# Routing written out in order, router logits in rounded parts, final norm inside the last expert, merging adds on VectorE

## Chip, cores and metric

One core of a Trainium2 chip. The time is that of one execution on the device, in microseconds (us). Engines are named as in the profile: PE is TensorE, DVE VectorE, ACT ScalarE, POOL GpSimd, SP SyncE; SPq and POOLq are the DMA queues that SyncE and GpSimd issue.

## What is computed

One layer of an encoder, all in float32, 1024 rows (tokens) of 1024 columns:

```python
xn = rms_norm(h, mix_norm_g);  p = xn @ w_in
merged = sum over b in (S5, RG-LRU, GLA) of sigmoid(gate_b) * (mixer_b(p_b) @ w_up_b)
h = h + merged @ w_mix_out
hn = rms_norm(h, ffn_norm_g)
probs = softmax(hn @ w_router)                 # 1024 x 16
gate, idx = lax.top_k(swapaxes(probs, 1, 2), 128)   # each expert takes its 128 best rows
xe = hn[idx]
hid = silu(xe @ w_exp_gate) * (xe @ w_exp_up)  # 1024 -> 2048
ye = (hid @ w_exp_down) * gate
h = h + scatter_add(idx, ye)
out = rms_norm(h, final_norm_g)
```

`rms_norm(h, g)` is `h * rsqrt(mean(h*h) + EPS) * g`, by row.

## The kernel before

A float32 product is made of three products of rounded parts: each operand is split into a high part `hi` (ScalarE's copy into the rounded type) and a low part `lo = x - hi` (VectorE), and `mm3` (L67 to L70) issues `hi*lo`, `hi*hi` and `lo*hi`. Weights are split in the kernel, in tiles of 128x1024, so each costs one ScalarE instruction (`xwh`) and one VectorE instruction (`xwl`).

**Mixers (to 712 us).** Projections and the three mixers; each branch is multiplied by its gate on VectorE and added into `merged` (8 tiles of 128x1024) by `gated` (L661 to L668), whose add went to GpSimd unless `eng` said VectorE. The order of this part is the framework's scheduler's. The LRU takes four blocks of columns through convolution, gates and scan on VectorE, with projections (`pj`) and its own products (`mx`) between them on TensorE.

**Output product (712 to 849).** `half(h, ...)` (L1075 to L1113) goes over the eight row tiles of 128 rows, once for the left 512 columns and once for the right: 24 matmuls of `mix` into `mo`, the add of the residual on VectorE, a write to `HACC` in device memory, squares with row sums on ScalarE, then four transposes `pt` and four float32 products `LG` with the router's weights `wr`. In the second half `route(t)` (L1178 to L1210) follows for each row tile: 12 instructions on 128x1 for the reciprocal root `rs`, the row scaled by it on ScalarE (`hn`), multiplied by the norm's gain `gff` on GpSimd and written to `HN` in device memory, and some 20 instructions of softmax on 128x16, the exponential by a polynomial. `prr` repeats each probability eight times and is transposed into `PT` (an expert in eight partitions).

**Search, slots, first gather (849 to 889).** Ten rounds (L1252 to L1262) find each expert's threshold: VectorE counts over the 1024 rows in `PT` (`junk`, 128x1024), TensorE sums the counts, VectorE sets the next digit. Between the rounds stand the parts of `probs` in bfloat16 (`aux`). Then come slot numbers (`sl`), the first expert's mask (128x1024), the product that turns it into row indices and gates, and the indirect read of its 128 rows from `HN` (`xe`).

**Experts (889 to 1986).** Sixteen experts, twelve operations each of 48 matmuls: `g` (gate), `u` (up), `d` (down) for four blocks of 512 columns, in the order of `SEQ` (L991 to L997). The instruction order is written by hand (`manual_schedule`, L1497 to L1525): `pre` and `post` hold what goes before and behind the matmuls of operation `i`, `NX` is the number of operations. During one operation the four weight tiles of the next are split. Weights come through 15 buffers of 1 MB (`rawa`, `rawb`, `rawc`), each loaded again once its split is done. The results of an expert are added to `HACC` by an indirect write.

**Final norm (1986 to 2015.8).** Four loads bring all of `HACC` back (`fin_load`), the last expert's rows are held apart. Behind the last operation `fin_sq`, `fin_rs`, `fin_out` (L1461 to L1478) go over pairs of row tiles: squares on ScalarE, 11 small instructions of reciprocal root on VectorE, the product with root and gain on VectorE or on ScalarE and GpSimd, the write to `out`. `row_add` adds the last expert's rows, `row_out` (L1485 to L1488) norms them and writes them by an indirect DMA of GpSimd's queue, over the plain rows.

Of the kernel before, what the change touches and what calls it, by code (L numbers as in the profile page):

```python
# [42 lines left out]
def hybrid_encoder(ctx: ExitStack, tc: tile.TileContext, A, out, dbg=None):  # L43
# [1031 lines left out]
    def half(h, H, w, pool, after):  # L1075

        def logits(t):
            pt = bank("pt")
            for j in range(4):
                te.transpose(pt[:, j * P:(j + 1) * P], H(t)[:, j * P:(j + 1) * P], idn)  # L1080
            hT = pool.tile([P, 4, P], F32, name="hT", bufs=2)
            act(hT.rearrange("p a b -> p (a b)"), pt, AF.Copy)
            yield
            for j in range(4):
                te.matmul(LG[:, t], hT[:, j], wr[:, 4 * h + j], start=False, stop=(h == 1 and j == 3),  # L1085
                          skip_group_check=True)
            yield

        lgen = rgen = iter(())
        for t in range(NT):  # L1090
            ps = bank("mo")
            mix(t, w, ps, 0, 2)
            next(lgen, None)
            mix(t, w, ps, 2, 4)
            next(lgen, None)
            if t:
                next(rgen, None)
                rgen = after(t - 1)
                next(rgen, None)
            mix(t, w, ps, 4, KT)  # L1100
            tt(v, H(t), ps, H(t), ADD)
            g.dma_start(HACC[t * P:(t + 1) * P, h * 512:(h + 1) * 512], H(t))
            sq = pool.tile([P, 512], F32, name="sq")
            act(sq, H(t), AF.Square, accum_out=ssq[:, h, t:t + 1])
            lgen = logits(t)
        with tc.manual_schedule():
            for _ in lgen:
                pass
            next(rgen, None)
            for _ in after(NT - 1):  # L1110
                pass

    half(0, lambda t: H0[:, t], wm[0], w0p, lambda t: iter(()))  # L1113
# [13 lines left out]
    bi_ = c2.tile([P, P], I32, name="bi")  # L1127
# [14 lines left out]
    aux = c2.tile([P, NE, NT, 5], BF, name="aux")  # L1142
# [35 lines left out]
    def route(t):  # L1178
        ss_, rs2, tm2, nm, sm_ = (w1p.tile(c1, F32, name=n, bufs=2) for n in ("ss2", "rs2", "tm2", "nm", "sm"))
        tt(v, ss_, ssq[:, 0, t:t + 1], ssq[:, 1, t:t + 1], ADD)  # L1180
        v.tensor_scalar(ss_, ss_, 1.0 / D, EPS, op0=MUL, op1=ADD)
# [394 lines left out]
```

## Time and profile before

| | |
|---|---|
| median of 3 runs | 2017.3 us (2012.62 to 2018.07) |
| profiled execution | 2017.55 us, span 2015.8 us |
| TensorE busy | 1883.6 us (93%) |
| VectorE busy | 1575.1 us (78%) |
| ScalarE busy | 1178.0 us (58%) |
| GpSimd busy | 211.7 us (11%) |
| mean rate of DMA | 246 GB/s |

The profile is of one execution. "Busy" counts the time in which an engine carries out instructions; a number in square brackets behind a row is the time that the engine stood idle before it, and what released it. The stages differ in which engine fills them, so the shares are read by stretch. The numbered groups of rows are further below.

### The profile page before, as it was taken

To read this page: it belongs to the slowest core of one execution; us is meant where nothing else is said; L and a number is where in the kernel's file an instruction comes from. 1 tells how busy PE (TensorE), PEld (TensorE's weight loads), DVE (VectorE), ACT (ScalarE), POOL (GpSimd) and SP (SyncE) were. 2 spreads that over 40 slices of the span, in tenths; PEclk is the share of its full clock that TensorE was granted. 3 is DMA by queue.
4 is the path that set the end of the run, shared out by engine and by line. 5 is a ranking of instruction groups with operands and counts; after the bars stand their busy time and mean duration, and the time that the engine had idled before them with its cause. 6 is when DMAs were issued, how large, how long until landed. Compare 5 with 4: busy or idle time off the path is not lost.

```text
span 2015.8 us, 25693 instructions
## 1 busy us (share of the span) xinstructions
PE 1883.6 (93%) x9502; PEld 1545.1 (77%) x9502; DVE 1575.1 (78%) x2162; ACT 1178.0 (58%) x1381; POOL 211.7 (11%) x227
## 2 busy tenths in 40 slices
PE   7999989999998998549999999999999999999994
PEld 6878866777777877438888888888888888888883
DVE  7467226558766245879999999999999999999997
ACT  5221234435574132327777778777777777777774
POOL 0834000002112102300000000000000000000001
PEclk9989999999999999869999999999999999999997
DMA  5431421302212162949999999999999999999972
GB/s 164 106 98 37 106 82 29 89 20 72 57 44 82 32 218 77 331 161 369 375 383 384 388 381 378 391 383 382 381 391 384 379 382 391 381 381 377 393 291 94
DMA packets 263233, 495.96 MB, mean 246 GB/s; under 512 B 26756, under 2 KB 82468, under 8 KB 263108
## 3 DMA queue, kind: packets, MB, share of 16 engines
q1 hardware_dynamic: 255924, 468.64, 64.4%
q0 software_dynamic: 7184, 25.69, 4.3%
q8 instruction: 74, 1.21, 0.2%
q14 instruction: 51, 0.42, 0.1%
HBM read 464.55 MB, written 29.74 MB: 245 GB/s over the span
## 4 chain that ended last, share of the span: by engine, by line
PE 77%; DVE 9%; ACT 3%; issue 2%; DMA 0%; SPq 0%; POOLq 0%; DVEq 0%; ACTq 0%
PE py L1379 17%; PE gu L68 12%; PE pj L380 12%; PE gu L70 12%; PE gu L69 12%; PE pj L390 3%; PE tp L1335 2%; PE mo L68 1%; PE mo L70 1%; PE mo L69 1%; DVE e L57 1%; DVE junk L1253 1%; DVE xc L57 1%; PE LG L1085 1%; PE mx L795 0%
## 5 line engine op out<-in xcount | busy, mean ns | idle before, releaser
L233 DVE TENSOR_TENSOR xwl<-rawb,xwh 128x1024 fp32r<-128x1024 f32 x528 | 613.7, 1218 | 20.4 <-ACT xwh L54 19.3
L54 ACT ACTIVATE xwh<-rawb 128x1024 fp32r<-128x1024 f32 x528 | 522.0, 1052 | 17.4 <-PE gu L70 7.5
L68 PE MATMUL gu<-xwl,xeh 128*128 128x512 f32 x1024 | 407.5, 398 | 0.0
L70 PE MATMUL gu<-xwh,xel 128*128 128x512 f32 x1024 | 400.3, 391 | 0.0
L69 PE MATMUL gu<-xwh,xeh 128*128 128x512 f32 x1024 | 399.1, 390 | 0.0
L233 DVE TENSOR_TENSOR xwl<-rawa,xwh 128x1024 fp32r<-128x1024 f32 x192 | 226.1, 1218 | 17.3 <-ACT xwh L54 17.3
L70 PEld LDWEIGHTS gu<-xwh,xel 128*128 128x128 f32 x1024 | 192.5, 188 | 41.9 <-DVE xel L62 0.3
L69 PEld LDWEIGHTS gu<-xwh,xeh 128*128 128x128 f32 x1024 | 193.1, 189 | 38.1
L68 PEld LDWEIGHTS gu<-xwl,xeh 128*128 128x128 f32 x1024 | 192.7, 188 | 37.4 <-ACT xeh L54 0.2
L54 ACT ACTIVATE xwh<-rawa 128x1024 fp32r<-128x1024 f32 x192 | 193.1, 1053 | 14.3 <-PE py L1379 5.1
L380 PE MATMUL pj<-xnL,wh 128*128 128x512 f32 x576 | 182.6, 396 | 5.5 <-DVE ev L57 2.0
L380 PE MATMUL pj<-xnH,wl 128*128 128x512 f32 x576 | 182.7, 397 | 1.8 <-DVE wl L62 1.8
L380 PE MATMUL pj<-xnH,wh 128*128 128x512 f32 x576 | 181.8, 394 | 0.0
L1379 PE MATMUL py<-xwl,hTh 128*128 128x512 f32 x512 | 159.3, 392 | 0.7 <-ACT hTh L54 0.7
L1379 PE MATMUL py<-xwh,hTh 128*128 128x512 f32 x512 | 158.0, 390 | 0.0
L1379 PE MATMUL py<-xwh,hTl 128*128 128x512 f32 x512 | 157.8, 389 | 0.0
L54 ACT ACTIVATE wh<-wraw 128x1024 fp32r<-128x1024 f32 (+2 forms) x60 | 49.6, 828 | 183.5 <-PE pj L380 124.0
L62 DVE TENSOR_TENSOR wl<-wraw,wh 128x1024 fp32r<-128x1024 f32 (+2 forms) x60 | 59.5, 992 | 108.7 <-ACT wh L54 97.0
L380 PEld LDWEIGHTS pj<-xnL,wh 128*128 128x128 f32 x576 | 108.4, 190 | 31.9 <-ACT ev L54 2.7
L380 PEld LDWEIGHTS pj<-xnH,wl 128*128 128x128 f32 x576 | 108.3, 190 | 27.9 <-DVE wl L62 3.6
L380 PEld LDWEIGHTS pj<-xnH,wh 128*128 128x128 f32 x576 | 108.8, 189 | 24.8 <-issue 1.8
L54 ACT ACTIVATE hTh<-tp 128x512 fp32r<-128x512 f32 x64 | 38.3, 599 | 125.8 <-PE tp L1335 125.8
(464 smaller groups left out, 2665.2 us busy)
## 6 DMA issues: line engine op xcount, KB each, us to landing
rawb<-in_w_exp_down_dram SPq DMA_DIRECT2D x90, 1024.0 KB, 9.4
rawb<-in_w_exp_up_dram SPq DMA_DIRECT2D x88, 1024.0 KB, 8.8
rawb<-in_w_exp_gate_dram SPq DMA_DIRECT2D x86, 1024.0 KB, 9.3
rawa<-in_w_exp_up_dram SPq DMA_DIRECT2D x40, 1024.0 KB
rawa<-in_w_exp_gate_dram SPq DMA_DIRECT2D x33, 1024.0 KB
rawa<-in_w_exp_down_dram SPq DMA_DIRECT2D x23, 1024.0 KB
wraw<-in_w_in_dram SPq DMA_DIRECT2D x36, 512.0 KB, 4.1
rawc<-in_w_exp_down_dram SPq DMA_DIRECT2D x15, 1024.0 KB
```

Of the source, the lines that this page charges most:

```text
L54: return s.activation(o, i, f, bias=bias, scale=scale, **k)
L57: return v.scalar_tensor_tensor(o, a, c, b, op0=op0, op1=op1)
L62: (eng or v).tensor_tensor(lo, src, h.bitcast(F32), SUB)
L68: te.matmul(ps, lh, rl, start=first, stop=False)
L69: te.matmul(ps, lh, rh, start=False, stop=False)
L70: te.matmul(ps, ll, rh, start=False, stop=last)
L233: e.tensor_tensor(o, a, b, op)
L380: te.matmul(ps[:, h], w[:, k], xx[:, k, h * 512:(h + 1) * 512], start=(k == 0 and i == 0), stop=(k == KT - 1 and i == 2))
L390: te.matmul(ps[:, h], ww[:, k], yy[:, h * 512:(h + 1) * 512], start=(k == 0 and i == 0), stop=(k == len(ys) - 1 and i == 2))
L1085: te.matmul(LG[:, t], hT[:, j], wr[:, 4 * h + j], start=False, stop=(h == 1 and j == 3), skip_group_check=True)
L1335: te.transpose(ps[:, j * P:(j + 1) * P], src[:, j * P:(j + 1) * P], idn)
L1379: te.matmul(E.py[:, h], a[:, j], b[:, h * 512:(h + 1) * 512], start=(f == 0 and j == 0 and p_ == 0), stop=(f == 3 and j == 3 and p_ == 2))
```

## The change

- `gated` adds into `merged` on VectorE, always.
- The router's weights and the transposed rows are split into rounded parts; `LG` has two halves per row tile, eight smaller products in place of four in float32.
- The second half of the output product is written out by hand. The norm's gain is multiplied on VectorE (`keep`), once for each half row, and `HN` gets rows without the reciprocal root, which is brought in later as a factor per row (`hrs`, its half, in the tanh; `rsq`, half its square, in `hid`). `norm` and `soft` work on four row tiles at once, for tiles 0 to 3 behind tile 4, and for 4 to 7 at the end. `parts` splits probability and root into three bfloat16 parts each, by casts on ScalarE. The first count of the search is made in two halves, one at tile 6.
- The search is written out by hand, without weight splits between its rounds; three of those go behind the first gather, one behind the first row splits. The second expert's mask moves from before the first gather's end into the first operation.
- The squares of the final norm go behind the last expert's operations, two a time behind `NX - 6` to `NX - 3`; the roots of all plain rows and the first output tile go ahead of operation `NX - 2`; the other output tiles are VectorE's. The last operation's four weight splits are shared between the last two operations.

The core of the diff, cut:

```diff
-    def gated(G, ps, j, first, eng=None):
+    def gated(G, ps, j, first):
...
-                tt(eng or g, m, m, G, ADD)
+                tt(v, m, m, G, ADD)
...
+    wr = c2.tile([P, KT, 2, NE], F32R, name="wr")
+    split(wr[:, :, 0], wr[:, :, 1], wr0)
...
+    def keep(t, h):
+        if not h:
+            hns[t] = w1p.tile([P, 2, 512], F32, name="hn", bufs=3)
+        tt(v, hns[t][:, h], (h0, h1)[h](t), gff[:, h * 512:(h + 1) * 512])
+        if h:
+            g.dma_start(HN[t * P:(t + 1) * P], hns[t].rearrange("p a b -> p (a b)"))
...
+        for t in range(NT):
+            ps = bank("mo")
+            mix(t, wm[1], ps, 0, 5)
+            next(lgen, None)
+            mix(t, wm[1], ps, 5, KT)
+            next(lgen, None)
+            if t == 6:
+                spread(slice(0, 4), prr)
+            keep(t, 0)
+            residual(t, 1, h1, ps, w1p)
+            keep(t, 1)
+            lgen = logits(t, 1, h1, w1p)
+            if t == 4:
+                norm(slice(0, 4))
+                prr = soft(slice(0, 4))
+            if t == 5:
+                for fn in parts(slice(0, 4), w1p):
+                    fn()
+            if t == 6:
+                v.tensor_scalar(junk0, PT[:, 0], cand.bitcast(F32), 0.0, op0=OP.is_ge, op1=ADD, accum_out=cnt0)
+        norm(slice(4, NT))
+        for _ in lgen:
+            pass
+        spread(slice(4, NT), soft(slice(4, NT)))
...
+            half_ = slice(1 if i == 0 else 0, 2)
+            v.tensor_scalar(junk[:, half_], PT[:, half_], cand.bitcast(F32), 0.0, op0=OP.is_ge, op1=ADD, accum_out=cnt)
...
+            if i:
+                tt(v, cur, cur, dig, OP.bitwise_or)
+                dig = tk.tile(c1, I32, name="dig", bufs=2)
+            for fn in late[2 * i:2 * i + 2]:
+                fn()
...
-        act(E.tg, E.pg, AF.Tanh, scale=0.5)
+        act(E.tg, E.pg, AF.Tanh, scale=E.hrs)
...
-        stt(E.hid, E.tg, 0.5, E.pu, MUL, MUL)
+        stt(E.hid, E.tg, E.rsq, E.pu, MUL, MUL)
...
-    EX[1] = sel_mask(1)
-    sel_mm(EX[1])
-    sel_idx(EX[1])
...
+        sel_gate(EX[0])
+        W = {0: [xlow(*z) for z in early_w[:3]]}
...
+    def fin_sq(t):
+        act(B_["j"], B_[t // 2][:, t % 2], AF.Square, accum_out=fs[:, t:t + 1])
+
+    def fin_out(t):
+        b_ = B_[t // 2][:, t % 2]
+        stt(b_, b_, fr[:, t:t + 1], B_["g"], MUL, MUL)
+        dma(out[0, t * P:(t + 1) * P], b_)
...
+            act(B_["j"][:, hs], E.yo[:, hs], AF.Square, accum_out=rsq[:, h:h + 1])
...
+    for t in range(NT):
+        at(post, NX - 6 + t // 2, fin_sq, t)
+    at(pre, NX - 2, fin_rs, slice(0, NT))
+    at(pre, NX - 2, fin_out, 0)
+    for t in (1, 2):
+        at(post, NX - 1, fin_out, t)
+    at(post, NX - 1, lambda: row_add(EX[NE - 1]))
+    for t in range(3, NT):
+        at(post, NX - 1, fin_out, t)
+    at(post, NX - 1, lambda: row_out(EX[NE - 1]))
...
-                while len(w) < 4:
+                while len(w) < (4 if i + 2 < NX else 2):
                     w.append(xsplit(i + 1, len(w)))
             w = W.pop(i)
+            while len(w) < 4:
+                w.append(xsplit(i, len(w)))
```

The order on the engines at two places. The first is VectorE in the second half of the output product: before, from the end of the fourth tile's routing over the fifth tile's add (`rawa<-mo`) to the next root; `e`, `sm` and `prr` belong to the softmax, `ss`, `rs` and `tm` to the root.

```order
L57 SCALAR_TENSOR_TENSOR e_6197<-e_6197,e_6195 128x16 x5
L1203 SCALAR_TENSOR_TENSOR e_6197,sm<-e_6197,ei 128x16
L1204 RECIPROCAL sm<-sm 128x1
L233 TENSOR_TENSOR rawa_5842<-mo,rawa_5842 128x512
L1206 TENSOR_SCALAR prr<-e_6197,sm 128x128
L1207 TENSOR_SCALAR probs<-e_6197,sm 128x16
L233 TENSOR_TENSOR ss_6258<-ssq 128x1
L1181 TENSOR_SCALAR ss_6258<-ss_6258 128x1
L73 TENSOR_SCALAR rs_6259<-ss_6258 128x1
L57 SCALAR_TENSOR_TENSOR tm_6260<-rs_6259 128x1
L76 TENSOR_TENSOR tm_6260<-tm_6260,ss_6258 128x1
```

After the change, from the end of the block for tiles 0 to 3 to the add of the following tile; `hTl` is the low part of transposed rows for the router, `hn` the row times gain.

```order
L1215 TENSOR_SCALAR ei<-e_6169 128x64
L1216 TENSOR_SCALAR e_6170<-e_6168 128x64
L57 SCALAR_TENSOR_TENSOR e_6170<-e_6170,e_6168 128x64 x5
L57 SCALAR_TENSOR_TENSOR e_6170<-e_6170,ei 128x64
L1221 TENSOR_REDUCE sm<-e_6170 128x4
L1222 RECIPROCAL sm<-sm 128x4
L233 TENSOR_TENSOR probs<-e_6170,sm 128x64
L1225 COPY prr<-probs 128x512
L62 TENSOR_TENSOR hTl<-pt,hTh 128x512
L233 TENSOR_TENSOR hn<-H_5412,gff 128x512
L233 TENSOR_TENSOR rawa_5893<-mo,rawa_5893 128x512
L233 TENSOR_TENSOR hn<-rawa_5893,gff 128x512
```

Between two adds there are now four wide instructions, and the small ones stand in two blocks.

The second place is ScalarE at the end. Before, from the last weight copies (`xwh`) on; `rawb` with `fs` is a square with its row sum, `rawb<-se` the final gain.

```order
L54 ACTIVATE xwh<-rawb_16342 128x1024 x2
L54 ACTIVATE xwh<-rawb_16397 128x1024 x2
L54 ACTIVATE xwh<-rawb_16399 128x1024 x2
L54 ACTIVATE hTh<-tp 128x512
L54 ACTIVATE rawb_16634<-se 128x512
L54 ACTIVATE rawb_16634,fs<-rawc_16490 128x1024 x2
L54 ACTIVATE rawb_16634,fs<-rawa_16492 128x1024 x2
L54 ACTIVATE rawc_16490<-rawc_16490,fr 128x1024
L54 ACTIVATE rawb_16634,fs<-rawa_16539 128x1024 x2
L54 ACTIVATE rawa_16492<-rawa_16492,fr 128x1024
L54 ACTIVATE rawb_16634,fs<-rawb_16541 128x1024 x2
L54 ACTIVATE rawa_16539<-rawa_16539,fr 128x1024
```

After the change, from the copies made in operation `NX - 4` to the end of the program:

```order
L54 ACTIVATE xwh<-rawb_16192 128x1024 x2
L54 ACTIVATE xwh<-rawa_16194 128x1024 x2
L54 ACTIVATE rawb_16487,fs<-rawa_16439 128x1024 x2
L54 ACTIVATE tg<-gu,fac 128x512
L54 ACTIVATE xwh<-rawa_16240 128x1024 x2
L54 ACTIVATE xwh<-rawb_16242 128x1024 x2
L54 ACTIVATE rawb_16487,fs<-rawb_16441 128x1024 x2
L54 ACTIVATE rawb_16487<-se 128x512
L54 ACTIVATE xwh<-rawb_16297 128x1024 x2
L54 ACTIVATE hTh<-tp 128x512
L54 ACTIVATE xwh<-rawb_16299 128x1024 x2
L54 ACTIVATE rawb_16487,rsq<-yo 128x512 x2
```

The squares stand between the weight copies; behind the last `xwh` only the squares of the last expert's rows are left. On VectorE, in the same way, `fin_out` of five tiles follows the last add, and the eight rows' root stands ahead of the last-but-one operation's splits. On TensorE, behind the last LRU product `mx`, the order has 51 and 36 matmuls `pj` before the first that reads the last `y`; after the change it has 13 and 36.

## Rows read from the trace of the kernel before

**Rows 1.** The page's chain that ended last, share of the span by engine.

```profile
PE 77%; DVE 9%; ACT 3%; issue 2%; DMA 0%; SPq 0%; POOLq 0%; DVEq 0%; ACTq 0%
```

**Rows 2.** Stretches (us): PE, PEld, DVE, ACT, POOL busy (instructions); PEclk, DMA, GB/s.

```profile
455.00:635.00 180.00, 163.31 (x676) 131.08 (x675) 131.25 (x126) 107.25 (x120) 26.66 (x17) 0.94 0.19 51
776.00:849.00 73.00, 53.48 (x265) 42.62 (x264) 60.80 (x256) 23.04 (x42) 27.57 (x23) 0.92 0.61 224
849.00:889.00 40.00, 6.36 (x52) 4.81 (x52) 28.95 (x85) 3.84 (x5) 1.04 (x1) 0.50 0.42 157
889.00:1980.40 1091.40, 1090.81 (x5080) 902.76 (x5079) 1038.14 (x1057) 845.47 (x938) 39.47 (x31) 1.00 1.00 371
1950.50:1980.40 29.90, 29.31 (x138) 24.12 (x136) 27.17 (x26) 22.36 (x26) 0.00 (x0) 1.00 0.11 44
1986.00:2015.80 29.80, 0.23 (x2) 0.00 (x0) 19.47 (x41) 8.38 (x13) 8.04 (x4) 0.58 0.39 158
```

**Rows 3.** Timeline of VectorE and GpSimd, LRU part: start, us, instruction [idle before].

```profile
458.31 2.36 DVE L869 TENSOR_SCALAR l<-l 128x8 f32<-128x8 f32 x1
...
503.68 2.51 POOL L233 TENSOR_TENSOR merged<-merged,ev 128x1024 f32<-128x1024 f32 x1 [12.22 <-DVE ev L57]
...
542.74 3.42 DVE L57 SCALAR_TENSOR_TENSOR li<-li,xc 128x1024 f32<-128x1024 f32 x1
```

**Rows 4.** The page's costliest groups: count | busy, mean ns | idle before.

```profile
L233 DVE TENSOR_TENSOR xwl<-rawb,xwh 128x1024 fp32r<-128x1024 f32 x528 | 613.7, 1218 | 20.4 <-ACT xwh L54 19.3
...
L54 ACT ACTIVATE xwh<-rawb 128x1024 fp32r<-128x1024 f32 x528 | 522.0, 1052 | 17.4 <-PE gu L70 7.5
```

**Rows 5.** Timeline of TensorE where it needs the last `y`.

```profile
628.55 0.80 PE L390 MATMUL pj<-y,wh 128*128 128x512 f32 x1 [7.19 <-DVE y L62]
```

**Rows 6.** Timeline of VectorE: row adds of the output product's halves.

```profile
753.55 0.69 DVE L233 TENSOR_TENSOR H<-mo,H 128x512 f32<-128x512 f32 x1 [6.25 <-PE mo L70]
...
774.45 0.69 DVE L233 TENSOR_TENSOR rawa<-mo,rawa 128x512 f32<-128x512 f32 x1 [6.34 <-PE mo L70]
...
838.74 0.67 DVE L233 TENSOR_TENSOR rawa<-mo,rawa 128x512 f32<-128x512 f32 x1
```

**Rows 7.** Timeline of VectorE: last routing and first count.

```profile
840.26 0.16 DVE L233 TENSOR_TENSOR ss<-ssq 128x1 f32<-128x1 f32 x1 [0.51 <-ACT sq L54]
...
849.08 1.28 DVE L1253 TENSOR_SCALAR_CACHE_REDUCE junk<-PT,cand 128x1024 bf16<-128x1024 f32 x1
```

**Rows 8.** Timeline of VectorE: search rounds, slots and first gather.

```profile
862.07 1.27 DVE L1253 TENSOR_SCALAR_CACHE_REDUCE junk<-PT,cand 128x1024 bf16<-128x1024 f32 x1
...
864.32 1.27 DVE L1253 TENSOR_SCALAR_CACHE_REDUCE junk<-PT,cand 128x1024 bf16<-128x1024 f32 x1
...
875.26 0.16 DVE L233 TENSOR_TENSOR cur<-cur,dig 128x1 int32<-128x1 int32 x1
...
878.62 0.29 DVE L57 SCALAR_TENSOR_TENSOR sl<-sl,sl 128x128 f32<-128x128 f32 x1
...
880.77 1.22 DVE L233 TENSOR_TENSOR tg<-islot,sl 128x1024 bf16<-128x1024 f32 x1
...
881.90 0.15 DVE L57 SCALAR_TENSOR_TENSOR idx<-ax 128x1 int32<-128x1 f32 x1
```

**Rows 9.** Timeline of ScalarE, VectorE and GpSimd at the end.

```profile
1982.00 1.06 ACT L54 ACTIVATE rawb<-rawc 128x1024 f32<-128x1024 f32 x1
...
1996.22 1.41 DVE L57 SCALAR_TENSOR_TENSOR yo<-py,gte,yo 128x512 f32<-128x512 f32 x2
...
2005.35 1.28 DVE L57 SCALAR_TENSOR_TENSOR yo<-yo,fr,rawb 128x1024 f32<-128x1024 f32 x1
...
2009.25 1.00 POOL L1487 DMA_INDIRECT out_dram<-yo,idx  x1 [9.48 <-issue]
```

**Rows 10.** Experts: VectorE's `hid` group; waits of SyncE's queue (us, times, longest).

```profile
L57 DVE SCALAR_TENSOR_TENSOR hid<-tg,gu 128x512 f32<-128x512 f32 x64 | 43.4, 679 | 0.0
...
SPq L1018 <- DVE xwl L233: 576.9, 229, 34.4
```

More of the change, by code (lines that the diff above doesn't have):

```diff
@@ L1073, in mix @@
             mm3(ps, MH[t][:, k], ML[t][:, k], w[0][:, k], w[1][:, k], k == 0, k == KT - 1)
[L1075 to L1111, printed above, removed]
@@ L1113, in hybrid_encoder, with logits @@
-    half(0, lambda t: H0[:, t], wm[0], w0p, lambda t: iter(()))
+    def logits(t, h, H, pool):
+        pt = bank("pt")
+        for j in range(4):
+            te.transpose(pt[:, j * P:(j + 1) * P], H(t)[:, j * P:(j + 1) * P], idn)
+        hh, hl = (pool.tile([P, 4, P], F32R, name=n) for n in ("hTh", "hTl"))
+        split(hh.rearrange("p a b -> p (a b)"), hl.rearrange("p a b -> p (a b)"), pt)
+        yield
+        for j in range(4):
+            w = wr[:, 4 * h + j]
+            te.matmul(LG[:, t].rearrange("p a e -> p (a e)"), hh[:, j], w.rearrange("p a e -> p (a e)"), start=False,
+                      stop=False, skip_group_check=True)
+            te.matmul(LG[:, t, 0], hl[:, j], w[:, 0], start=False, stop=(h == 1 and j == 3), skip_group_check=True)
+        yield
@@ L1208, in route, with spread @@
-        yield
-        te.transpose(PT[:, t // 4, (t % 4) * P:(t % 4 + 1) * P], prr.rearrange("p e j -> p (e j)"), idn)
-    half(1, lambda t: H1[t // 4][:, t % 4], wm[1], w1p, route)
+        tt(v, probs[:, c], e2, sm_[:, :, None].to_broadcast(wide))
+        prr = w1p.tile([P, n, NE, 8], F32, name="prr")
+        v.tensor_copy(prr, probs[:, c, :, None].to_broadcast([P, n, NE, 8]))
+        return prr
+    def spread(c, prr):
+        for i, t in enumerate(range(c.start, c.stop)):
+            te.transpose(PT[:, t // 4, (t % 4) * P:(t % 4 + 1) * P], prr[:, i].rearrange("p e j -> p (e j)"), idn)
@@ new lines, in parts @@
+    def parts(c, pool):
+        n = c.stop - c.start
+        wide = [P, NE, n]
+        rem = pool.tile(wide, F32, name="rem")
+        rem8 = pool.tile([P, n], F32, name="rem8")
+        pr = probs[:, c].rearrange("p t e -> p e t")
+        cast = lambda i, z: (lambda: act(aux[:, :, c, i], z, AF.Copy))
+        w8 = lambda z: z[:, None, :].to_broadcast(wide)
+        return [cast(2, pr), lambda: tt(v, rem, pr, aux[:, :, c, 2], SUB), cast(3, rem),
+                lambda: tt(v, rem, rem, aux[:, :, c, 3], SUB), cast(4, rem),
+                cast(5, w8(hrs[:, c])), lambda: tt(v, rem8, hrs[:, c], aux[:, 0, c, 5], SUB), cast(6, w8(rem8)),
+                lambda: tt(v, rem8, rem8, aux[:, 0, c, 6], SUB), cast(7, w8(rem8))]
@@ new lines, in hybrid_encoder @@
+    cnt0 = c2.tile([P, 1], F32, name="cnt0")
+    junk0 = w1p.tile([P, 512], BF, name="junk0")
+    with tc.manual_schedule():
+        lgen = iter(())
+        for t in range(NT):
+            ps = bank("mo")
+            mix(t, wm[1], ps, 0, 5)
+            next(lgen, None)
+            mix(t, wm[1], ps, 5, KT)
+            next(lgen, None)
+            if t == 6:
[13 more added lines that the diff above has]
+        norm(slice(4, NT))
+        for _ in lgen:
+            pass
+        spread(slice(4, NT), soft(slice(4, NT)))
@@ L1314, in sel_mm, with sel_gate @@
         for t in range(NT):
[L1315 removed]
+            te.matmul(E.ps[:, 0:8], E.oh[:, t], aux[:, E.e, t], start=(t == 0), stop=(t == NT - 1))
     def sel_idx(E):
[L1318 to L1319 removed]
+        ax = ew.tile([P, 2], F32, name="ax", bufs=2)
+        v.tensor_copy(ax, E.ps[:, 0:2])
         E.idx = ew.tile([P, 1], I32, name="idx", bufs=4)
[L1321 to L1325 removed]
+        stt(E.idx, ax[:, 0:1], 128.0, ax[:, 1:2], MUL, ADD)
+    def sel_gate(E):
+        fac = ew.tile([P, 3], F32, name="fac", bufs=4)
+        v.tensor_reduce(fac[:, 0:2], E.ps[:, 2:8].rearrange("p (a b) -> p a b", b=3), axis=mybir.AxisListType.X, op=ADD)
+        stt(fac[:, 2:3], fac[:, 1:2], 2.0, fac[:, 1:2], MUL, MUL)
+        E.gate, E.hrs, E.rsq = (fac[:, i:i + 1] for i in range(3))
     def gather(E):
```

209 lines of the change are left out of this document (99 added, 110 removed).

## The prediction

> **What bounds the kernel now.** I began with the chain of waits and the table of stretches, and then read, stretch by stretch, which wait ends last. The chain is TensorE for 77% of the span and VectorE for 9% [rows 1]. The table says where the two alternate [rows 2]. In the experts (889 to 1980) TensorE is busy 1090.8 of 1091.4 us, so that stretch only shrinks if its matmuls do, and they don't. VectorE is nearly full there as well, 1038.1 us. All that can be won lies elsewhere: in the LRU part (455 to 635) TensorE idles 16.7 of 180 us, in the second half of the output product with its routing (776 to 849) 19.5 of 73, in the threshold search and the first gather (849 to 889) 33.6 of 40, and behind the last matmul all of 29.8.
>
> The sum is made against the profiled execution, 2017.55 us, which is 0.25 over the median of 2017.3 (2012.6 to 2018.1). What a measurement can tell from no change is about 0.3%, 6 us.
>
> **A. Merging adds on VectorE.** Fourteen adds leave GpSimd, eight of them in the LRU part, 2.51 us each there. While one runs, an instruction of VectorE stands still: seven are stretched between 458.31 (a 128x8 form, 2.36 us) and 542.74 (3.42 us, where a full 128x1024 form takes 1.22, as the subtractions of the weight split do) [rows 3, 4]. Taking each against its plain form gives 13.6 us of VectorE lost; the eighth add lengthened nothing. In its place VectorE runs eight adds of about 1.21, 9.7 us. Net it is freed of 3.9. The six later adds lie where TensorE hardly waits and count as nothing. The same edit makes the scheduler place TensorE's matmuls otherwise: behind the last LRU product 49 matmuls stand before TensorE needs the last `y`, where 87 stood. That wait is 7.2 us now [rows 5]. With 38 fewer at 163.3/676 = 0.24 us each [rows 2] it would grow by 9.2; but the matmuls now stand earlier, where the remaining 9.5 of the 16.7 us are idle, so what counts is how soon VectorE gets there. I take its own relief, **-4 us**; the ends are +5.3 (9.2 exposed, 3.9 saved) and -12 (most of the idle time goes).
>
> **B. Second half and routing.** In the first half, without routing, VectorE waits 6.25 and adds 0.69: a row tile takes 6.94 us. In the second half seven tiles take 838.74 - 774.45 = 64.3 us, because each routing of some 36 small instructions stands on VectorE ahead of the next tile's add [rows 6]. Now four tiles are routed at once, twice. Tiles 0 to 3 and 5 to 7 lose nothing to it: four 0.7-us instructions of VectorE per tile fit into 6.94. Behind tile 4 stand 13 instructions of the norm and 22 of the softmax, ahead of the `hTl` that TensorE's router products of that tile need. A 128x1 instruction takes 0.16, a 128x128 one 0.29 [rows 7, 8]; for 128x4 I take 0.2 with the gap behind it, for 128x64 0.24. That is 2.6 + 5.3, with a lead of 1.5 from the add (838.74 to 840.26, as before) and 0.7 for `hTl` 10.1 us behind the add; TensorE asks for it at 6.2, a stall of 3.9. The half count placed at tile 6 costs 0.5. So the last add comes at 774.45 + 48.6 + 3.9 + 0.5 = 827.4. From there again 1.5 + 2.6 + 0.7 + 5.3, and 1.7 for the copy and four transposes: the first count starts at 839.2, against 849.08 now [rows 7]. With 0.4 for the router products behind `hTl`: **-9.5**. Each of the 22 wide forms may be 0.065 less or more (0.16 to 0.29 without the gap), twice: 6.6 to 12.4. The gathered rows go out unnormalised: no scaling on ScalarE and no GpSimd multiply ahead of their write. That was no last wait, and counts zero; if the write came late, the first gather would wait, and it has over 30 us.
>
> **C. Search.** It takes 849.08 to 875.42, 26.3 us; a clean round is 864.32 - 862.07 = 2.25 [rows 7, 8], ten make 22.5, so four low-part subtractions among the rounds cost 3.8. They leave: three go beside the gather, one behind the first splits. The first count covers half the columns, 0.6 of its 1.27. The remainders on VectorE add 0.3. One new wait: the cast of the second remainder stands on ScalarE behind six weight copies of 1.05 [rows 4], ready 6.9 us after the probabilities where VectorE asks at 5.0 (the round's own wait for TensorE hides 0.2): 1.7, between 0 and 6.3. Sum **-2.4** (+2.2 to -4.1).
>
> **D. First gather.** The second expert's 128x1024 mask stands between the first expert's copy and its index, 880.77 to 881.90 [rows 8], and moves into the first operation: -1.1, and 0.4 back for wider selection products. **-0.7**. The mask is 1.2 us more for VectorE in an operation whose first weights are split already: it is covered by the lead over TensorE; without this it would cost 1.2.
>
> **E. End.** ScalarE's eight squares move from behind the experts into four operations, two in each. They take 1.06 apiece with their accumulator read on top [rows 9]. In the last operations ScalarE is busy 22.4 of 29.9 us [rows 2], 1.4 free an operation where 2.1 to 2.5 come in. VectorE gets the reciprocal roots of all rows (2.2) and one output row (1.28) ahead of the last operation's weights. I let the last matmul be **3.4 us late**, between 0 and 8.5 (all squares exposed). What is left behind it, on VectorE: the add of the last rows 1.4, five output rows of 1.28, twelve instructions of 0.2 for the root, one more row of 1.28 [rows 9], with 0.2 to start, 11.7 us. GpSimd's scattered write starts when the plain rows have landed: today 2.6 after VectorE's end, then about as VectorE ends, and from its start to the span's end it is 2015.8 - 2009.25 = 6.55. Together 18.3 instead of 29.8 [rows 2]: 11.5 less 3.4, **-8.1** (-3 to -11.5).
>
> **Experts.** Gate and norm factor are read as per-row factors; the counts of instructions don't change, and the sixteen experts count zero. Their cover is VectorE's 53.3 free us.
>
> Sum: 4 + 9.5 + 2.4 + 0.7 + 8.1 = 24.7; 2017.55 - 24.7 = **1993 us**.
>
> **Rivals.**
> *The last LRU block lies open.* The cover of 49 matmuls is too short and nothing earlier gets shorter: A is +5.3, 9.3 worse, **2002**. For it speaks the 7.2-us wait that exists already; against it, that VectorE is only 131 of 180 us busy there.
> *VectorE cannot take the adds.* If stretched instructions were mere waiting time that VectorE had to spare, the eight adds are 9.7 us more on its path: A is +9.7, **2007**. The stretched forms stand in the middle of the gate chains, which speaks against it. The Trainium skill ("Perfetto Trace Analysis", Optimizing Scalar/DVE Operations) would have it so for a saturated VectorE: handing work to ScalarE or even GpSimd may then make sense. The same place warns that these two share an SBUF port so that moving between them might not help, and the 3.42 us bear that half out.
> *The weights set the pace.* The DMA engines count as fully busy in the experts, 371 GB/s [rows 2]. If the rate of loading were the limit, an earlier start would only drain the buffers, and B, C and D (12.6) vanish: **2006**. Against it: the queue that issues the loads waits 576.9 us for VectorE to free a buffer [rows 10], so it is held back, not behind.
> *The end isn't shortened.* The squares saturate ScalarE and all 8.5 us come back before the last matmul: E is -3, **1998**.
> *Slower: the experts' `hid`.* The one per-operation edit on a nearly full engine is the factor that `hid` now reads per row. It takes 0.68 us, 64 times [rows 10]. VectorE's 53.3 free us are used up from 0.83 more apiece; at three times its time (+1.36, 87 us) the experts grow by 34, **2027**. Against it: the end's add, which reads such a factor and the same kind of operand, takes 1.41 for two [rows 9], no more.
>
> **How the numbers follow.** Forecast 0.54, with its own range 1985 to 2000 from the ends of B, C and E, which won't all fall on one side; last block open 0.16; end not shortened 0.12; weights 0.08; adds 0.07; `hid` 0.03. The range takes all but the last and part of the outer ones: 1983 to 2007. All but the last are faster by over 6 us, though several at once come near: faster 0.94, same 0.03, slower 0.03.
>
> **What would show it.** In the changed profile: no VectorE instruction over 2.3 us between 455 and 635, and the wait before the last `y`, which A says stays under 12 us; row adds of the second half 6.9 apart but for one 4 us longer; a first count near 835, both gains of A and B together; one round of the search 1.7 us longer than the rest and no subtraction among them; experts of 1091 us or with 3 to 4 us lost in the last three operations; some 18 us behind the last matmul. Wrong would be: idle TensorE in the middle of the experts, or a second half with stalls at every tile.

## The result and the profile after

The changed kernel takes 1992.2 us (1991.8 to 1994.3, 4 runs) against 2017.6 us, a ratio of 0.988 (0.987 to 0.989). 1993 was forecast. The execution that was profiled took 1994.3 us, with a span of 1992.5; spans are compared below, 2015.8 - 1992.5 = 23.3 us.

The chain of the changed kernel and its stretches, cut where the stages now lie (columns as in [rows 2]):

```profile
PE 80%; DVE 6%; ACT 3%; issue 1%; DMA 1%; SPq 0%; POOLq 0%; DVEq 0%; ACTq 0%
```

```profile
455.00:635.00 180.00, 162.90 (x692) 130.36 (x692) 129.29 (x135) 107.50 (x121) 0.54 (x8) 0.96 0.21 57
771.09:838.00 66.91, 55.14 (x272) 46.19 (x271) 35.85 (x108) 14.77 (x33) 8.64 (x16) 0.87 0.72 262
838.00:872.35 34.35, 3.80 (x36) 2.56 (x35) 25.74 (x78) 6.45 (x10) 1.48 (x1) 0.50 0.26 97
872.35:1961.00 1088.65, 1088.65 (x5079) 901.08 (x5080) 1040.35 (x1058) 855.22 (x948) 40.53 (x31) 1.00 1.01 374
1974.51:1992.50 17.99, 0.00 (x1) 0.00 (x0) 10.48 (x20) 1.34 (x4) 0.98 (x1) 0.60 0.48 193
```

TensorE is 80% of the chain where it was 77% [rows 1]. Its idle time in the LRU part is as large as before, 17.1 of 180 us. In the routing it is 11.8 us where it was 19.5 [rows 2], in the experts (to 1961) nothing, and 18.0 us lie behind the last matmul. Before, the last matmul ended at 1986.2, with 29.6 us behind it; the row of [rows 2] is cut at 1986.0.

TensorE's wait for the last `y` (timeline) is 13.2 us, where it was 7.2 [rows 5]:

```profile
623.91 2.07 PE L390 MATMUL pj<-y,wh 128*128 128x512 f32 x4 [13.21 <-DVE y L62]
```

The same five landmarks in both traces put each term beside its forecast. A is read at the first row add of the second half, B at the search's first count, C at the end of the search, D at the first transposes of the gathered rows, E behind that (last matmul 2.8 late, end 11.6 shorter):

| term | landmark before | after | gain, us | forecast |
|---|---|---|---|---|
| A | 774.45 | 771.09 | 3.4 | 4.0 |
| B | 849.08 | 838.00 | 7.7 | 9.5 |
| C | 875.42 | 860.84 | 3.5 | 2.4 |
| D | 886.82 | 872.35 | -0.1 | 0.7 |
| E | 2015.8 | 1992.5 | 8.8 | 8.1 |
| sum | | | 23.3 | 24.7 |

Timeline of VectorE in the second half, the adds of tiles 3 to 7, the wait for the last router products and the first count (start, us, instruction, [idle before]):

```profile
790.74 0.69 DVE L233 TENSOR_TENSOR rawa<-mo,rawa 128x512 f32<-128x512 f32 x1
...
797.59 0.69 DVE L233 TENSOR_TENSOR rawa<-mo,rawa 128x512 f32<-128x512 f32 x1
...
807.93 0.69 DVE L233 TENSOR_TENSOR rawa<-mo,rawa 128x512 f32<-128x512 f32 x1
...
817.55 0.69 DVE L233 TENSOR_TENSOR rawa<-mo,rawa 128x512 f32<-128x512 f32 x1
...
824.81 0.69 DVE L233 TENSOR_TENSOR rawa<-mo,rawa 128x512 f32<-128x512 f32 x1
...
831.35 0.23 DVE L1205 COPY lg<-LG 128x64 f32<-128x64 f32 x1 [1.75 <-PE LG L1089]
...
838.00 0.75 DVE L1317 TENSOR_SCALAR_CACHE_REDUCE junk<-PT,cand 128x512 bf16<-128x512 f32 x1 [1.21 <-PE PT L1230]
```

TensorE's stand at tile 4 and its granted clock around it (timeline, then a table of stretches):

```profile
807.47 0.38 PE L1089 MATMUL LG<-wr,hTl 128*128 128x16 f32 x1 [3.05 <-DVE hTl L62]
```

```profile
797.59:804.40 6.81, 6.81 (x36) 5.60 (x35) 5.98 (x29) 1.32 (x3) 1.08 (x2) 1.00 1.03 352
807.47:811.00 3.53, 3.53 (x12) 3.14 (x13) 2.40 (x5) 1.60 (x5) 1.08 (x2) 0.50 1.05 403
811.00:815.00 4.00, 4.00 (x14) 3.10 (x13) 0.33 (x2) 1.69 (x4) 0.00 (x0) 0.62 1.05 400
815.00:817.55 2.55, 2.55 (x17) 2.17 (x14) 1.29 (x2) 0.60 (x1) 0.00 (x0) 1.00 1.04 406
```

Tile 4's products wait 3.05 us for `hTl`, as B said (3.9). But the next 7.5 us run at a granted clock of 0.50 and 0.62 of full speed, so tile 6's add comes 9.62 behind tile 5's, where 6.86 is the pace of tiles 2 to 4. Nothing of that was in the sum.

The second round of the search, on VectorE, and the gather on GpSimd:

```profile
839.71 1.28 DVE L1317 TENSOR_SCALAR_CACHE_REDUCE junk<-PT,cand 128x1024 bf16<-128x1024 f32 x1
...
842.80 0.28 DVE L233 TENSOR_TENSOR rem<-rem,aux 128x64 f32<-128x64 f32 x1 [1.54 <-ACT aux L54]
...
843.43 1.28 DVE L1317 TENSOR_SCALAR_CACHE_REDUCE junk<-PT,cand 128x1024 bf16<-128x1024 f32 x1
...
845.62 1.28 DVE L1317 TENSOR_SCALAR_CACHE_REDUCE junk<-PT,cand 128x1024 bf16<-128x1024 f32 x1
```

```profile
867.28 1.48 POOL L1397 DMA_INDIRECT xe<-HN,idx  x1 [40.22 <-DVE fac L1391]
```

The round lasts 3.72 where a clean one lasts 2.19, with 1.54 idle for the cast (1.7 forecast). GpSimd's indirect read starts 0.8 behind the index and takes 1.48.

The end: TensorE's two late waits, then VectorE and GpSimd.

```profile
1966.80 0.70 PE L1447 MATMUL py<-xwl,hTh 128*128 128x512 f32 x2 [2.25 <-DVE xwl L233]
...
1968.45 0.79 PE L1447 MATMUL py<-xwh,hTl 128*128 128x512 f32 x1 [0.38 <-DVE hTl L62]
```

```profile
1974.55 1.41 DVE L57 SCALAR_TENSOR_TENSOR yo<-py,fac,yo 128x512 f32<-128x512 f32 x2 [1.50 <-PE py L1447]
...
1984.16 1.28 DVE L57 SCALAR_TENSOR_TENSOR yo<-yo,fr,rawb 128x1024 f32<-128x1024 f32 x1
```

```profile
1986.05 0.98 POOL L1559 DMA_INDIRECT out_dram<-yo,idx  x1 [65.92 <-DVE yo L57]
```

Last matmul at 1974.5, last row at 1985.4, scattered write at 1986.05 and the end 6.45 behind it: 18.0 (18.3 forecast).

### The profile page after: what moved, and what is told of

Same layout as the page of the kernel before. It is cut to its first block, busy times and chain, and to the rows that moved or that the text cites. A ratio compares the mean times of both kernels' runs of the same rounds, so it can differ in the third digit from the quotient of the medians.

```text
span 1992.5 us, 25512 instructions
## 1 busy us (share of the span) xinstructions
PE 1879.4 (94%) x9502; PEld 1542.6 (77%) x9502; DVE 1553.8 (78%) x2018; ACT 1174.8 (59%) x1377; POOL 145.5 (7%) x202
## 4 chain that ended last, share of the span: by engine, by line
PE 80%; DVE 6%; ACT 3%; issue 1%; DMA 1%; SPq 0%; POOLq 0%; DVEq 0%; ACTq 0%
PE py L1447 17%; PE pj L380 12%; PE gu L68 12%; PE gu L70 12%; PE gu L69 12%; PE pj L390 3%; PE tp L1403 2%; PE mo L68 2%; PE mo L69 1%; PE mo L70 1%; DVE junk L1317 1%; DVE lr L934 0%; PE mx L795 0%; PE mx L802 0%; ACT gt L54 0%
## 5 line engine op out<-in xcount | busy, mean ns | idle before, releaser
L54 ACT ACTIVATE xwh<-rawb 128x1024 fp32r<-128x1024 f32 x528 | 522.1, 1053 | 13.6 <-PE gu L70 7.0
L1447 PEld LDWEIGHTS py<-xwh,hTl 128*128 128x128 f32 x512 | 96.4, 188 | 21.1 <-DVE hTl L62 0.9
```

The lines of the kernel that those rows point to most:

```text
L54: return s.activation(o, i, f, bias=bias, scale=scale, **k)
L1447: te.matmul(E.py[:, h], a[:, j], b[:, h * 512:(h + 1) * 512], start=(f == 0 and j == 0 and p_ == 0), stop=(f == 3 and j == 3 and p_ == 2))
```

## The experiments

Each median stands with that of the kernel before, measured beside it, since that one lies between 2016.5 and 2017.9 us from one group of runs to the next. Run 5 is the changed kernel once more, in one group with runs 6 to 8.

**1. The merging adds back on GpSimd.**

```diff
-    def gated(G, ps, j, first):
+    def gated(G, ps, j, first, eng=None):
...
-                tt(v, m, m, G, ADD)
+                tt(eng or g, m, m, G, ADD)
...
-            gated(G, U_, j, False)
+            gated(G, U_, j, False, v if j >= 6 else None)
```

> The changed kernel with the merging adds back on GpSimd, as before; TensorE's order in the LRU part is then the old one too. In the changed kernel the last y comes 4.6 us earlier than before (623.91 against 628.55) and the first row add of the output's second half 3.4 earlier (771.09 against 774.45). If the adds are what that came from, both go back: 1995.6 us, seven VectorE instructions stretched to over 2.3 us, last y near 628.5. Rival, the gain came from elsewhere in the change (the smaller router products, the tiles' new room): within 0.5 us of 1992.2.

1996.5 us (before 2016.5), ratio 0.990 (0.988 to 0.991): some 4 us given back. Timeline of VectorE, then of TensorE where it needs the last `y`:

```profile
458.58 2.36 DVE L869 TENSOR_SCALAR l<-l 128x8 f32<-128x8 f32 x1
...
504.15 3.41 DVE L57 SCALAR_TENSOR_TENSOR xc<-xcl,cols,xc 128x1024 f32<-128x1024 f32 x1
...
543.08 3.42 DVE L57 SCALAR_TENSOR_TENSOR li<-li,xc 128x1024 f32<-128x1024 f32 x1
```

```profile
628.95 1.65 PE L390 MATMUL pj<-y,wh 128*128 128x512 f32 x3 [7.19 <-DVE y L62]
```

The stretched instructions are back in their places [rows 3], and `y` is late again. The first row add of the second half comes at 774.28. The adds, with the order of TensorE's matmuls that goes with them, are what A came from.

**2. Only the adds moved, in the kernel before.**

```diff
-                tt(eng or g, m, m, G, ADD)
+                tt(v, m, m, G, ADD)
```

> The kernel before with nothing but the merging adds put on VectorE; TensorE's order in the LRU part is then the changed kernel's. If term A stands alone: 3.4 us below before, 2014.2, with the first row add of the second half near 771. Rival, the exposed last block: the wait for the last y grows to 13 or more and the time is as before or above, 2017 to 2019.

2014.7 us (before 2016.5), ratio 0.9989 (0.9980 to 0.9998): 1.7 us, half of what was expected, where the rival expected no gain. Timeline of TensorE at the last `y`:

```profile
624.19 2.08 PE L390 MATMUL pj<-y,wh 128*128 128x512 f32 x4 [13.21 <-DVE y L62]
```

`y` comes 4.4 us sooner than before although the wait for it is 6 longer [rows 5], but the first row add only 1.4 sooner (773.03). From this point to that add it is 145.3 to 145.9 us in the three traces with a wait of 7.1 or 7.2 (before, runs 1 and 11) and 146.7 to 148.8 in the ten with 13.2. The difference does not lie at the wait for `y`: from there to the first row add of the first half it is 92.9 to 94.1 us in all thirteen. It lies at the start of the output product, where TensorE waits 2.7 or 2.8 us for `MH` in all of them; the second row add then comes 3.0 to 3.7 us behind the first in the three and 4.0 to 6.1 in the ten. Timeline of TensorE there in this run, and stretches behind that wait in this run (two) and in the kernel before:

```profile
708.58 0.80 PE L68 MATMUL mo<-wml,MH 128*128 128x512 f32 x1 [2.74 <-ACT MH L54]
```

```profile
708.58:712.60 4.02, 4.02 (x9) 2.94 (x10) 4.02 (x5) 4.02 (x5) 0.00 (x0) 0.50 1.05 398
712.60:716.60 4.00, 4.00 (x14) 3.13 (x14) 4.00 (x5) 2.61 (x3) 0.00 (x0) 0.73 1.11 321
712.40:714.50 2.10, 1.88 (x7) 1.27 (x8) 2.10 (x2) 2.10 (x3) 0.00 (x0) 1.00 1.05 402
```

The granted clock behind the wait was 0.50 and 0.73 here and 1.00 before. Part of A's gain goes there, a different part in each execution; why the ten and not the three is not shown.

**3. The softmax of tiles 0 to 3 behind the split of tile 4.**

```diff
             next(lgen, None)
+            if t == 5:
+                prr = soft(slice(0, 4))
             mix(t, wm[1], ps, 5, KT)
...
-                prr = soft(slice(0, 4))
```

> The changed kernel with one move: the softmax of tiles 0 to 3 goes behind the low part of tile 4's transposed rows, so that TensorE's router products of tile 4 no longer wait for it. In the changed kernel TensorE stands 3.05 us at tile 4, and the stretch behind that shows a granted clock of 0.50 and 0.62 where it was 1.00, with tile 6's add 9.6 behind tile 5's instead of 6.9. If the slow tile is the clock after the stall, both go: 3.05 + 0.4 + 2.7, some 6 us less, 1986.2, all row adds 6.9 apart. Rival, the half count and the casts that I placed there cost the second part (the prediction's 0.5 too low): only 3 to 3.5 go, 1989, and the add of tile 6 stays 9 us behind.

1995.5 us (before 2016.5), ratio 0.989 (0.988 to 0.991): a miss for both expectations, some 2.5 us slower than run 5 and 3 slower than the changed kernel's first measurement. Timeline of TensorE and a table of stretches:

```profile
809.62 0.66 PE L1081 MATMUL pt<-idn,rawa 128*128 128x128 f32 x4 [1.49 <-DVE rawa L233]
...
814.56 0.28 PE L1087 MATMUL LG<-wr,hTh 128*128 128x32 f32 x1 [2.20 <-ACT hTh L54]
...
815.28 0.38 PE L1089 MATMUL LG<-wr,hTl 128*128 128x16 f32 x1 [0.44 <-DVE hTl L62]
```

```profile
804.50:808.10 3.60, 3.60 (x16) 2.66 (x15) 3.15 (x16) 0.00 (x0) 0.00 (x0) 1.00 1.04 409
816.00:820.00 4.00, 4.00 (x15) 3.52 (x15) 1.88 (x4) 0.72 (x2) 1.08 (x2) 0.50 1.04 418
```

The wait at tile 4 is gone, and two others stand at tile 5: tile 5's row add is now behind the softmax (1.49), and the high part of its transposed rows on ScalarE is behind the casts of `parts` (2.20, and 0.44 more for the low part). Then comes the half-speed stretch again. The stall had been moved, not taken away.

**4. The early weight copies behind the casts.**

```diff
-    early_w = [xhigh(n // 4, n % 4) for n in range(XB)]
+    early_w = []
...
+            if i == 3:
+                early_w = [xhigh(n // 4, n % 4) for n in range(XB)]
```

> The changed kernel with the six early weight copies on ScalarE moved behind the casts of the search's fourth round. Round two of the search lasts 3.72 us against 2.19, with VectorE idle 1.54 for a cast behind those copies. If the copies are the cause the round goes to 2.2 and the time falls by 1.5, to 1990.7; the first gather's cover isn't touched since the copies take 6.2 us and have until 866. Rival, the copies late make the three subtractions beside the gather late: nothing gained or up to 3 us lost in the first operation.

1992.2 us (before 2016.5), ratio 0.988 (0.986 to 0.989). Timeline of VectorE, the second and third count:

```profile
838.31 1.28 DVE L1317 TENSOR_SCALAR_CACHE_REDUCE junk<-PT,cand 128x1024 bf16<-128x1024 f32 x1
...
840.50 1.28 DVE L1317 TENSOR_SCALAR_CACHE_REDUCE junk<-PT,cand 128x1024 bf16<-128x1024 f32 x1
```

The second round is as long as the others, 2.19 (838.31 to 840.50), and from first count to the end of the search it is 1.5 less; the cause of that wait is shown. The median is 0.8 under run 5 and equal to the first measurement, a difference too small for these runs. Part of the gain came back: from the first transposes of the gathered rows to the end it is 1121.4 us here and 1121.0 in run 9, which moves the copies too, and 1120.2 and 1120.5 in the two traces of the changed kernel.

**5. The changed kernel again.**

> The changed kernel itself, beside the three that follow: 1992 us. Its slow tile (9.62 us from tile 5's add to tile 6's) should come out somewhat differently, since the same tile took 8.16 in the run with the copies behind the casts, whose order there is the same; if the half-speed stretch behind a stall varies between executions, so does this tile by about 1.5 us. Rival: the placement of the copies changed it, and it is 9.6 again.

1993.0 us (before 2016.5), ratio 0.9885 (0.987 to 0.990). Tile 6's add comes 8.17 behind tile 5's, with the same order that gave 9.62.

**6. The softmax in two pieces.** `soft` becomes a generator that stops behind `ei`; both `next` calls stand behind a tile's split; the casts of tiles 0 to 3 go into search rounds five to nine.

```diff
+            if t == 5:
+                sgen = soft_(slice(0, 4))
+                next(sgen)
+            if t == 6:
+                prr = next(sgen)
+            if t == 7:
+                spread(slice(0, 4), prr)
+                v.tensor_scalar(junk0, PT[:, 0], cand.bitcast(F32), 0.0, op0=OP.is_ge, op1=ADD, accum_out=cnt0)
             mix(t, wm[1], ps, 5, KT)
...
-                for fn in parts(slice(0, 4), w1p):
-                    fn()
```

> The changed kernel with the softmax of tiles 0 to 3 cut into two pieces, each put directly behind the low part of a tile's transposed rows (tiles 4 and 5), the first count's left half and the transposes before it at tile 7, and the casts of the parts of tiles 0 to 3 moved into the later search rounds. In the run with the softmax in one piece behind the split, TensorE waited 1.49 us for the late row add, and 2.20 for a high part that stood behind the casts on ScalarE, and half speed followed. If stall and half speed are the whole loss, no wait of TensorE is left between tiles 4 and 7, the row adds are 6.9 apart, and some 6 us go: 1986. Rival, the routing's work itself is what the tiles pay for and moves with it: another wait appears and the gain is under 2 us.

1987.0 us (before 2016.5), ratio 0.986 (0.984 to 0.987): 6.0 us under run 5, as expected. Stretches from tile 4's add to tile 7's:

```profile
795.68:804.84 9.16, 9.16 (x50) 7.65 (x50) 6.81 (x29) 1.32 (x3) 1.08 (x2) 1.00 1.00 369
804.84:812.16 7.32, 7.32 (x40) 6.19 (x39) 5.08 (x16) 1.32 (x3) 1.08 (x2) 1.00 1.05 403
812.16:816.84 4.68, 4.68 (x29) 3.96 (x27) 3.26 (x8) 1.32 (x3) 1.08 (x2) 1.00 1.04 400
```

TensorE is busy throughout, at full speed. The stall and the slow stretch behind it were all that B lost against its sum, and more: from first row add to first count it is 60.2 us here, 66.9 and 65.4 in the two traces of the changed kernel, and 74.6 before. (VectorE's adds are 9.2, 7.3 and 4.7 apart, since pieces of the softmax stand before two of them; nothing waits for that.)

**7. The root behind the last splits.**

```diff
-    at(pre, NX - 2, fin_rs, slice(0, NT))
-    at(pre, NX - 2, fin_out, 0)
-    for t in (1, 2):
+    at(post, NX - 1, fin_rs, slice(0, NT))
+    for t in (0, 1, 2):
```

> The changed kernel with the root of the plain rows and the first output row moved on VectorE from before the last operation's splits to behind them. Now TensorE waits 2.25 and 0.38 us there. If VectorE is what sets the end from there on, its work is the same and only its idle 1.5 us before the last rows' add can go: 1990.7, while the last matmul ends 2.6 earlier. Rival, by my sum, which put the late last matmul into the end in full: 2.6 less, 1989.5.

1992.1 us (before 2016.5), ratio 0.988 (0.986 to 0.989): 0.9 less than run 5, where 1.5 was expected and 2.6 by the rival. Timeline of TensorE's only late wait and of VectorE's last add and last row:

```profile
1963.73 0.73 PE L1447 MATMUL py<-xwl,hTh 128*128 128x512 f32 x2 [0.69 <-ACT hTh L54]
```

```profile
1972.75 1.40 DVE L57 SCALAR_TENSOR_TENSOR yo<-py,fac,yo 128x512 f32<-128x512 f32 x2
...
1982.36 1.28 DVE L57 SCALAR_TENSOR_TENSOR yo<-yo,fr,rawb 128x1024 f32<-128x1024 f32 x1
```

The 2.25 and 0.38 us are gone, the last matmul ends at 1969.6, and the last add comes 3.1 us behind it, straight after VectorE's plain rows: VectorE sets the end, and of TensorE's 2.6 us no more than VectorE's own idle time, 1.5, could be won. From the first transposes to the end it is 1120.1 us, against 1120.2 and 1120.5 in the two traces of the changed kernel, so what was won is under 1 us.

**8. The final norm as before.** `fin_sq`, `fin_rs`, `fin_out` and their calls are those of the kernel before, behind the last operation.

> The changed kernel with the final norm as before: squares, roots and output rows behind the last operation, half of them by ScalarE and GpSimd. Term E alone is undone: 29.8 us behind the last matmul in place of 18.0, the last matmul 2.6 earlier, so 9.2 more, 2001.4. Rival, the end wasn't shortened by the moved squares and the time came from the rest: under 4 more, below 1996.

2000.5 us (before 2016.5), ratio 0.992 (0.991 to 0.994): 7.5 over run 5. From the last matmul to the end it is 29.6 us again, and in the last operations TensorE waits only the 0.7 us for `hTh` that stood there before too. E is shown, a little smaller than expected (9.2) and than read off the traces (8.8). The run brings back the moved squares and GpSimd's multiplies together, so it does not say what each is worth; one of VectorE's output rows is again held up beside such a multiply (1.28 alone):

```profile
1982.06 3.30 DVE L57 SCALAR_TENSOR_TENSOR rawa<-rawa,fr,rawb 128x1024 f32<-128x1024 f32 x1
```

**9. Three moves together** (those of runs 4, at the ninth round, 6 and 7).

> The changed kernel with three moves together: the softmax of tiles 0 to 3 in two pieces (6.0 less alone), the six early weight copies behind the search's ninth round (1.5 less in the search, alone 0.8 in the time), and the root of the plain rows behind the last splits (0.9 less alone). If they are independent, 7.7 less than the changed kernel's 1993.0: 1985.3. Rival, the copies that late hold up the subtractions beside the gather and the gain of the search is given back: 1986.5 or more.

1986.2 us (before 2017.9), ratio 0.985 (0.983 to 0.986). By the ratios it is 7.7 under run 5 (0.9885 - 0.9847), as expected, by the medians 6.8. Faster than both kernels; against run 6 alone (0.986) the two small moves can't be told from nothing.

**10. Nothing beside the gather.**

```diff
-        W = {0: [xlow(*z) for z in early_w[:3]]}
...
-        W[0].append(xlow(*early_w[3]))
+        W = {0: [xlow(*z) for z in early_w[:4]]}
```

> The changed kernel with the three subtractions of weight splits taken away from beside the first gather and put behind the first row splits. From the index's end to TensorE's first use of the rows took 4.8 us before (882.05 to 886.82) and takes 5.9 in the changed kernel (866.46 to 872.35), where GpSimd's indirect DMA starts 0.8 after the index and is 1.48 us long in place of 1.04. If VectorE's subtractions hold GpSimd up, it goes back to 4.8 with 1.04, while the first operation pays for the late subtractions, 1 to 3 us over the changed kernel: 1994 to 1996. Rival, the unnormalised rows' late write or the longer wait for the factors makes the gather slow: it stays 5.9.

1997.6 us (before 2017.9), ratio 0.990 (0.988 to 0.991): above the 1994 to 1996 expected, by the ratios 2.2 over run 5. TensorE waits 2.6 us for the late subtractions at its first operation. Timeline of GpSimd, then of TensorE:

```profile
867.87 1.02 POOL L1397 DMA_INDIRECT xe<-HN,idx  x1 [40.20 <-DVE fac L1391]
```

```profile
872.46 0.88 PE L1403 MATMUL tp<-idn,xe 128*128 128x128 f32 x3 [5.84 <-DMA xe<-HN,idx]
```

Without the three subtractions beside it GpSimd's instruction takes 1.02 again, and from the index's end (867.06) to the rows' use it is 5.4: half of the lost 1.1 us is the doing of VectorE's subtractions. The instruction still starts 0.8 behind the index, where 0.3 was enough before; why, stays open.

**11. The merging adds left out.**

```diff
-                tt(v, m, m, G, ADD)
+                pass
```

> The changed kernel without the fourteen merging adds: each branch's product with its gate is still made, but the merged rows hold the first branch alone. In the LRU part VectorE has eight adds of 1.2 us less, 9.7. If VectorE's own work sets the last y, as term A says, y comes up to 9.7 us sooner than in the changed kernel (622 to 624, after a wait of 13.2), so 612 to 618, and the time falls by 5 to 10. Rival, latency sets it (scan, gates and products in turn, with VectorE free in between): y moves by under 2 us and the gain is under 3.

1981.7 us (before 2017.9), ratio 0.982 (0.981 to 0.984): 11.3 under run 5, more than the 5 to 10 expected. Timeline of TensorE at the last `y`:

```profile
614.88 2.07 PE L390 MATMUL pj<-y,wh 128*128 128x512 f32 x4 [7.12 <-DVE y L62]
```

Eight adds, 9.7 us of VectorE, and `y` is 9.0 us sooner than in the changed kernel (7.1 than in run 5). Part of that spread lies ahead: the LRU part's instruction at L869 starts anywhere from 454.7 to 460.1 us in the thirteen traces, and none of runs 3 to 10, which span that range, edits anything ahead of it. Counted from there, `y` comes 170.2 and 170.4 us later with the adds on GpSimd (before, run 1), 164.5 to 166.0 in the ten with the adds on VectorE, and 156.3 here, 8.2 sooner than in the changed kernel and in run 5 alike. VectorE's work sets the last `y`, though VectorE is busy only 129 of those 180 us. The rest of the 11.3 lies behind the wait for `MH` (run 2).

## Why the prediction was right, point by point

**A**, 4.0 forecast, 3.4 seen. Runs 1, 2 and 11 bear out the mechanism: what VectorE does ahead of the last `y` sets when `y` comes, if not one for one. Counted from L869, `y` is 4.2 to 5.9 us sooner for a relief that I put at 3.9, with TensorE's order changed too, and 8.2 sooner for 9.7 (run 11). The "last block lies open" was half true, and its price was not: the wait for `y` did grow from 7.2 to 13.2, past the 12 that I had given as the sign of A, but the other waits of that part shrank from 9.5 to 3.9, and `y` itself came 4.6 sooner. What the step missed is that 1 to 3 us are lost again behind the wait for `MH` (run 2). "VectorE cannot take the adds" is refuted by the same runs, in an odd way. VectorE is what this part waits for, so the rule of the Trainium skill ("Perfetto Trace Analysis", Optimizing Scalar/DVE Operations) on a saturated VectorE seems to apply; but GpSimd's eight adds cost it 13.6 us of standing still and eight of its own cost 9.7. The warning behind that rule, that VectorE and GpSimd share an SBUF port and moving work between them might not help, is the half that agrees with these numbers.

**B**, 9.5 forecast, 7.7 seen, the term with the largest miss. Tile 4's stall was priced well (3.05 in TensorE's wait, 3.9 forecast). The step that failed is "Tiles 0 to 3 and 5 to 7 lose nothing to it". Tile 6's add came 2.7 late, and run 6, with no stall, shows all adds at full speed: half speed behind the stall was the reason. It was not the half count, which starts at 818.89, behind that add; the 0.5 set down for it came as 0.4, between the adds of tiles 6 and 7 (7.26 for 6.86). Another 1.0 went behind tile 7 (1.75 us for the router products, where 0.4 was allowed), and 1.0 came back since the first tile of the half has no router products ahead of it (5.94).

The sum does not depend on why the tiles were slow before, but that reading was incomplete. Timeline of GpSimd and VectorE in the kernel before, at one row tile:

```profile
789.03 2.40 POOL L233 TENSOR_TENSOR hn<-hn,gff 128x1024 f32<-128x1024 f32 x1 [3.71 <-ACT hn L54]
```

```profile
789.06 2.39 DVE L1199 TENSOR_SCALAR e<-e 128x16 f32<-128x16 f32 x1
```

A 128x16 form of this kind takes 0.17 alone. In each of the eight tiles one instruction of VectorE lasts in this way until GpSimd's multiply by the gain ends, as with the adds of A: 14.6 us over the seven tiles, of the 15.7 by which their 64.3 exceed the first half's pace. The prediction put it all down to the small instructions, and counted the multiply that leaves GpSimd as zero. The two half-row products that VectorE makes in its place take 0.69 each, 9.7 for seven tiles. By these rows I estimate that some 5 us of B come from taking the multiply off GpSimd and the rest from routing four tiles at once; no run separates the two.

**C**, 2.4 forecast, 3.5 seen. The wait for the cast is there, 1.54 (1.7 forecast), and run 4 shows its cause. The rest was too cautious: a round is 2.19 where 2.25 was carried over from before, since `cur` is no longer in the way, and the remainders cost nothing that can be seen.

**D**, 0.7 forecast, -0.1 seen. From the search's end the index is 1.0 us sooner, and from there to the rows' use it is 1.1 slower (5.9 where it was 4.8). The sum counted the subtractions beside the gather as free; run 10 shows that they lengthen GpSimd's instruction by 0.46.

**E**, 8.1 forecast, 8.8 seen, the tail itself 18.0 against 18.3. The last matmul is late, but by the root and the output row on VectorE, not by ScalarE's squares, which I had named with them; and run 7 shows that this lateness costs under 1 us, not its full 2.8, since VectorE sets the end. Overlooked here too were GpSimd's multiplies, three in the old end; the last of them and the output row of VectorE beside it, in the kernel before:

```profile
1997.43 2.35 POOL L233 TENSOR_TENSOR rawa<-rawa,rawb 128x1024 f32<-128x1024 f32 x1 [3.05 <-ACT rawa L54]
```

```profile
1997.55 3.31 DVE L57 SCALAR_TENSOR_TENSOR rawa<-rawa,fr,rawb 128x1024 f32<-128x1024 f32 x1
```

Three instructions of VectorE took 2.27, 2.20 and 3.31 us there in place of 0.17, 0.17 and 1.28, which is 6.2 of the 11.6 us by which the end became shorter; the moved squares are not all of it.

**The other rivals.** The weights don't set the pace: experts that started 14.5 us sooner took as long as before, apart from the late waits. `hid` became 0.06 us longer (0.742 against 0.679), 4 us of VectorE's free 53.

So the total came out within 1 us of the median partly by luck: the terms erred with both signs, -0.6, -1.8, +1.1, -0.8 and +0.7 (gain seen less forecast), and the profiled execution, in which they were read, lies 2.2 us above the median.

## What to carry to other kernels

When a block of small instructions is moved, list every instruction behind it on its engine and ask which other engine needs each: run 3 moved one stall into two, run 6 cut the block so that it stood only behind what TensorE needed next, and won 6 us. Look at what VectorE does beside each large GpSimd instruction: one of 2.4 us held up a VectorE instruction of 0.17 to its end, in three stages of this kernel. Price a wait of TensorE with what follows it: behind the wait of 3.05 us at tile 4 another 1.3 to 2.8 were lost at half speed. And a wait taken from one engine is worth only what the engine that sets the end gets back: 2.6 us of TensorE's were worth less than 1.

## What was not expected of the hardware

The stretch at half speed behind the same stall differs between executions of the same order: in the eight profiled executions with that order at these tiles, tile 6's add came 9.62, 9.64 and 9.71 behind tile 5's in three, and 8.16 to 8.18 in five, never between. At the start of the experts the granted clock was 0.50 too, and its mean over the next 30 us was 0.95 and 0.90 in two executions of the changed kernel. So single executions of one kernel differ by 1 to 3 us in places that have nothing to do with an edit, and by up to 5.4 where the LRU part starts (run 11); two of my expectations (in runs 4 and 9) were of that size. The profiles show how the clock stood, not why the stretch is longer in some executions; that was not tried.
